# A looped ScalarE, lora_E on SyncE's queue, three idle matmuls and a moved pause in an AdaLoRA forward kernel

## The chip, the cores and the metric

The kernel runs on one core of a Trainium2 chip. Its time is the device time of one execution in microseconds (us): before the change the median of 3 runs is 161.67 us (161.62 to 162.06). A core has five engines that run by themselves and meet at semaphores: TensorE (PE in the profile, with its weight loads as PEld), VectorE (DVE), ScalarE (ACT), GpSimd (POOL) and SyncE (SP). SyncE and ScalarE issue transfers (DMAs) between the chip's main memory and the core's on-chip memory; 16 DMA engines carry them.

## The reference

```python
x_flat = x.reshape(-1, in_dim)          # x: 16 x 2048 x 256, f32
y = x_flat @ W                          # W: 256 x 256
lora_out = x_flat @ lora_A              # lora_A: 256 x 16
lora_out = lora_out * lora_E            # lora_E: 16
lora_out = lora_out @ lora_B            # lora_B: 16 x 256
y = y + scale * lora_out                # scale = 1.0
```

So 32768 rows of 256 numbers are read (33.5 MB), multiplied by a 256 x 256 matrix with a low-rank term added, and 33.5 MB are written.

## The kernel before, in words

The low-rank term is folded into the weights once: lora_A is transposed by TensorE (L171), scaled by lora_E on VectorE (L175), multiplied by lora_B (L180) and added to W, in bf16 (`weff`, L184). After that one multiplication by `weff` gives y.

The rows of x are cut into five blocks. A block of b rows a partition is a tile of 128 partitions x b x 256 in on-chip memory; `PLAN` gives b as 56, 56, 48, 48, 48. There is room for three blocks (three slots, of 56, 56 and 48 rows), and y is written over x in the same place, so blocks 3 and 4 can be loaded only after stores 0 and 1 have landed. A block is loaded in two or three pieces, each with its own semaphore, and stored by one transfer.

Work goes in 32 steps of 8 rows a partition (7 for each of the first two blocks, 6 for each of the rest). Step t is: VectorE rounds x to bf16 (`rounded`, L159); TensorE transposes it as 8 f32 blocks, two bf16 numbers in each f32 word (`transposed`, L198); VectorE copies the transposed block out of PSUM (`copied`, L163); TensorE multiplies it by `weff` in two halves of 8 matmuls (`multiplied`, L209); ScalarE copies each half out of PSUM over x (L232). TensorE runs its steps in a loop of 16 turns of two; ScalarE's 64 copies are written out one by one, each waiting for the count of finished halves in `s_m`.

All loads of x and all stores are issued by SyncE, in this order: W, load 0, load 1, load 2, store 0, store 1, load 3, load 4, store 2, store 3, store 4. Each store waits for ScalarE's copy of the block's last half (`s_y`); some issues wait for more: store 1 for 30 finished halves (`ISSUE_PRODUCTS`, L245), load 3 for store 0 and load 4 for store 1 to have landed, load 4 also for 20 transposed steps (`ISSUE_LOAD`, L250), store 3 for 29 (`ISSUE_STORE`, L243). ScalarE issues the three small loads of lora_A, lora_B and lora_E at the front.

VectorE holds the whole compute back once (`HOLD`, L151 to L158): ahead of step 16 it runs ten no-operations, waits until store 0 has landed, and then makes five copies into a spare tile, each waited for.

```python
HOLD = 16, 0, 5        # step, store that is waited for, spare copies
```

Of the kernel before, what the change touches and what calls it, by code (L numbers as in the profile page):

```python
# [4 lines left out]
PLAN = [56, 56, 48, 48, 48]  # L5

PIECES = {0: [16, 16, 24], 1: [16, 16, 24], 2: [24, 24], 3: [24, 24], 4: [24, 24]}

SLOTS = [56, 56, 48]
LEAD = 3  # L10
AFTER = {1: [3, 4]}

HOLD = 16, 0, 5


ISSUE_LOAD, ISSUE_STORE = {4: 20}, {3: 29}
ISSUE_PRODUCTS = {1: 30}

S, G = 8, 4
P = 128  # L20
FP32 = mybir.dt.float32
# [16 lines left out]
def kernel(tc, x, W, lora_A, lora_B, lora_E, scale, out):  # L38
    nc = tc.nc
    x_flat = x.flatten_outer_dims()  # L40
    out_flat = out.flatten_outer_dims()
    N, K = x_flat.shape
    M = out_flat.shape[1]
    R = lora_B.shape[0]
# [4 lines left out]
    steps = [(i, r) for i, b in enumerate(PLAN) for r in range(0, b, S)]  # L49
    NS = len(steps)  # L50
    assert NS % 2 == 0

    def rows_of(flat, i):
        b, r0 = PLAN[i], starts[i]
        return flat[r0:r0 + b * P, :].rearrange("(p b) k -> p b k", b=b)

    def sbuf(name, shape, dt):
        return nc.alloc_sbuf_tensor(name, shape, dt).ap()

    def psum(name, shape, dt):  # L60
        return nc.alloc_psum_tensor(name, shape, dt).ap()

    slots = [sbuf(f"xy{s}", [P, rows, K], FP32) for s, rows in enumerate(SLOTS)]
    a_sb = sbuf("a_sb", [P, KC, R], FP32)
    e_sb = sbuf("e_sb", [R, 1], FP32)
    w_sb = sbuf("w_sb", [P, KC, M], FP32)
    b_sb = sbuf("b_sb", [R, M], FP32)
    b_bf = sbuf("b_bf", [R, M], BF16)
# [3 lines left out]
    ident = sbuf("ident", [P, P], FP32)  # L72
# [7 lines left out]
    ps_y = [psum(f"psum_y{k}", [P, G, M], FP32) for k in range(2)]  # L80
# [4 lines left out]
    s_w, s_a, s_b, s_e = (Count(nc, f"s_{k}") for k in "wabe")  # L85

    pieces = {}
    for i, b in enumerate(PLAN):
# [1 line left out]
        pieces[i] = [(sum(parts[:j]), n) for j, n in enumerate(parts)]  # L90
    s_ld = {(i, r): Count(nc, f"s_ld{i}_{r}") for i in pieces for r, n in pieces[i]}
    s_st = [Count(nc, f"s_st{i}") for i in range(len(PLAN))]
    s_id, s_set, s_v, s_t, s_m, s_y = (
        Count(nc, k) for k in ("s_id", "s_set", "s_v", "s_t", "s_m", "s_y"))
    tick = nc.alloc_semaphore("tick")


# [2 lines left out]
    can_y = [[nc.alloc_semaphore(f"can_y{h}_{k}") for k in range(2)] for h in range(S // G)]  # L100

    def slot(i):
        return slots[i % LEAD][:, :PLAN[i], :]

    opening = []

    def transfer(queue, count, **aps):
        ins = queue.dma_start(**aps)
        for names in opening:
            names.add(ins.ins.name)  # L110
        count.by(ins, 16)

    def load(i):
        for r, n in pieces[i]:
            transfer(nc.sync, s_ld[i, r], out=slot(i)[:, r:r + n, :], in_=rows_of(x_flat, i)[:, r:r + n, :])

    def store(i):
        transfer(nc.sync, s_st[i], out=rows_of(out_flat, i), in_=slot(i))

    def spent(engine, count):  # L120
        engine.wait_ge(count.sem, count.total).then_inc(count.sem, -count.total)

    def take(sem):
        nc.tensor.wait_ge(sem, 1).then_inc(sem, -1)
# [4 lines left out]
    transfer(nc.sync, s_w, out=w_sb, in_=W.rearrange("(p c) m -> p c m", c=KC))  # L129
    transfer(nc.scalar, s_a, out=a_sb, in_=lora_A.rearrange("(p c) r -> p c r", c=KC))  # L130
    transfer(nc.scalar, s_b, out=b_sb, in_=lora_B)
    transfer(nc.scalar, s_e, out=e_sb, in_=lora_E[:, None])
    load(0)
    opening.clear()
    tc.close()
# [1 line left out]
    for i in range(1, LEAD):  # L137
# [5 lines left out]
        out=ident, in_=ident, compare_op=mybir.AluOpType.not_equal, fill=1.0, base=0,  # L143
# [3 lines left out]
    def rounded(t):  # L147
        i, r = steps[t]
        if (i, r) in s_ld:
            nc.vector.wait_ge(s_ld[i, r].sem, 16)  # L150
        if t == HOLD[0]:  # L151

            for _ in range(10):
                nc.vector.engine_nop()
            nc.vector.wait_ge(s_st[HOLD[1]].sem, 16)
            for _ in range(HOLD[2]):
                nc.vector.tensor_copy(out=spare, in_=slot(i)[:, r:r + 2 * S, :]).then_inc(tick, 1)  # L157
                nc.vector.wait_ge(tick, 1).then_inc(tick, -1)  # L158
        nc.vector.tensor_copy(out=xb[t % 2], in_=slot(i)[:, r:r + S, :]).then_inc(can_t[t % 2], 1)  # L159

    def copied(t):
        nc.vector.wait_ge(s_t.sem, t + 1)
        nc.vector.tensor_copy(out=xt[t % 2], in_=ps_xt[t % 2]).then_inc(can_m, 1)  # L163


    nc.vector.wait_ge(s_b.sem, 16)
    s_v.by(nc.vector.tensor_copy(out=b_bf, in_=b_sb))  # L167
    nc.tensor.wait_ge(s_a.sem, 16)
    nc.tensor.wait_ge(s_id.sem, 2)
    for c in range(KC):  # L170
# [4 lines left out]
    s_v.by(nc.vector.tensor_scalar(  # L175
        out=ate, in0=ps_at, scalar1=e_sb, scalar2=float(scale),
        op0=mybir.AluOpType.mult, op1=mybir.AluOpType.mult))
    nc.tensor.wait_ge(s_v.sem, 2)
    for c in range(KC):
        aeb_done = nc.tensor.matmul(ps_aeb[:, c, :], ate[:, c, :], b_bf, start=True, stop=True)  # L180
    s_set.by(aeb_done)
    nc.vector.wait_ge(s_w.sem, 16)
    nc.vector.wait_ge(s_set.sem, 2)
    s_v.by(nc.vector.tensor_add(out=weff, in0=w_sb, in1=ps_aeb))  # L184
    rounded(0)
    rounded(1)
    for t in range(NS):
        copied(t)
        if t + 2 < NS:
            rounded(t + 2)  # L190
# [12 lines left out]
    def multiplied(k):  # L203
        take(can_m)
        for h in range(S // G):
            nc.tensor.wait_ge(can_y[h][k], 1)
            for j in range(G):
                for c in range(KC):
                    done = nc.tensor.matmul(  # L209
                        ps_y[h][:, j, :], pairs[k][:, h * G + j, :, c], weff[:, c, :],  # L210
                        start=(c == 0), stop=(c == KC - 1))
                if j == 0:
                    done.then_inc(can_y[h][k], -1)
            done.then_inc(s_m.sem, 1)

    transposed(0)
    nc.tensor.wait_ge(s_v.sem, 3)
# [1 line left out]
    with nc.tensor.Fori(0, NS // 2):  # L219
        for k in range(2):  # L220
            transposed(1 - k)
            multiplied(k)
    s_t.total, s_m.total = NS + 1, NS * S // G

    for h in range(S // G):
        nc.scalar.sem_inc(can_y[h][0], 1)
    n = 0
    for i, r in [(i, r + g) for i, r in steps for g in range(0, S, G)]:
        n += 1
        nc.scalar.wait_ge(s_m.sem, n)  # L230
        t, h = divmod(n - 1, S // G)
        y = nc.scalar.copy(out=slot(i)[:, r:r + G, :], in_=ps_y[h])  # L232
        free = can_y[h][(t + 1) % 2]
        if r + G < PLAN[i]:
            y.then_inc(free, 1)
        else:
            done = s_y.by(y)
            if n < s_m.total:
                nc.scalar.wait_ge(s_y.sem, done)
                nc.scalar.sem_inc(free, 1)  # L240
            nc.sync.wait_ge(s_y.sem, done)
            if i in ISSUE_STORE:
                nc.sync.wait_ge(s_t.sem, ISSUE_STORE[i])  # L243
            if i in ISSUE_PRODUCTS:
                nc.sync.wait_ge(s_m.sem, ISSUE_PRODUCTS[i])  # L245
            store(i)
            for later in AFTER.get(i, []):
                nc.sync.wait_ge(s_st[later - LEAD].sem, 16)
                if later in ISSUE_LOAD:
                    nc.sync.wait_ge(s_t.sem, ISSUE_LOAD[later])  # L250
                load(later)


    for count in [s_a, s_id]:
# [1 line left out]
    spent(nc.tensor, s_v)  # L256
    for count in [s_b, s_e, s_w, s_set] + list(s_ld.values()):
        spent(nc.vector, count)
    spent(nc.scalar, s_m)
    nc.tensor.wait_ge(can_y[0][NS % 2], 1).then_inc(can_y[0][NS % 2], -1)  # L260
    for count in [s_y, s_t] + s_st:
        spent(nc.sync, count)

# [34 lines left out]
```

## Time and profile before

| what | value |
|---|---|
| median of 3 runs | 161.67 us |
| the profiled execution | 161.75 us |
| its span, first to last instruction | 160.4 us |
| moved | 67.42 MB, 420 GB/s over the span |
| busy: PE, DVE, ACT | 57%, 55%, 39% |
| VectorE waits for store 0 at the hold | 19.0 us, until 70.6 |
| first copy of ScalarE, last copy | from 16.4, from 131.1 us |

Times in the profile are counted from the start of the span. In the page's second part the span is cut into 40 slices of 4.0 us; a digit is the busy share of a slice in tenths, and GB/s is what the DMA engines moved. The third part has one row for each DMA queue: packets, megabytes, share of 16 engines' span; q1 is SyncE's queue, q10 is ScalarE's, q14 carries instructions. In a table by windows each row gives the stretch, its length, busy us and instructions (x) of PE, PEld, DVE, ACT and POOL, then the granted TensorE clock, the DMA share and GB/s. A row of waits reads: who waited, for whom, us in total, times, longest. A row of the timeline reads: start, us, engine, line, operation, how many.

### The profile page before, as it was taken

The numbers are of one execution on the slowest core, as the hardware profiler recorded it, in microseconds if no ns is written. First come the engines' busy times: TensorE is split into PE (matmuls) and PEld (weight loads), VectorE is DVE, ScalarE is ACT, GpSimd is POOL, SyncE is SP. The second block draws the span as 40 slices with busy tenths as digits, with TensorE's granted clock in tenths as the row PEclk, the third lists the DMA queues.
The fourth block names the chain that finished last, engine by engine and source line by source line (L and its number), as shares of the span: only waits on it lengthen the run. The fifth ranks groups of instructions, "written<-read, shape, count | busy, mean of one in ns | idle before, by whom it ended". The sixth has DMA issues, their size and how long they took to land. (4 is left out here: it accounts for less than half of the span.)

```text
span 160.4 us, 1883 instructions
## 1 busy us (share of the span) xinstructions
PE 91.8 (57%) x780; PEld 82.7 (52%) x780; DVE 87.9 (55%) x72; ACT 63.2 (39%) x65; POOL 0.7 (0%) x6
## 2 busy tenths in 40 slices
PE   0149999999999600000009999999999960000000
PEld 0028889999999500000008999999999950000000
DVE  0187769998988000039999669899898500000000
ACT  1100675868676700000001768686868670000000
POOL 1000000000000000000000000000000000000000
PEclk9999999999999975555555999999999999555555
DMA  5999999999999999999989999999999999999994
GB/s 179 409 433 447 429 415 433 449 435 411 466 404 392 458 457 457 457 443 457 415 386 382 423 404 460 411 455 423 496 404 404 466 453 429 404 417 490 429 429 196
DMA packets 2802, 67.42 MB, mean 420 GB/s; under 512 B 480, under 2 KB 496, under 8 KB 624
## 3 DMA queue, kind: packets, MB, share of 16 engines
q1 hardware_dynamic: 2592, 67.37, 98.0%
q10 hardware_dynamic: 208, 0.03, 0.2%
q14 instruction: 2, 0.02, 0.0%
HBM read 33.85 MB, written 33.55 MB: 420 GB/s over the span
## 5 line engine op out<-in xcount | busy, mean ns | idle before, releaser
L232 ACT COPY xy<-psum_y 128x1024 f32<-128x1024 f32 x64 | 61.9, 1017 | 65.5 <-PE psum_y L209 65.5
L209 PE MATMUL psum_y<-weff,xt 128*128 128x256 bf16 x512 | 63.7, 280 | 0.1
L209 PEld LDWEIGHTS psum_y<-weff,xt 128*128 128x128 bf16 x512 | 51.4, 101 | 7.1 <-issue 0.3
L198 PE MATMUL psum_xt<-ident,xb 128*128 128x128 f32 x264 | 36.8, 287 | 31.3 <-DVE xb L159 31.3
L198 PEld LDWEIGHTS psum_xt<-ident,xb 128*128 128x128 f32 x264 | 31.9, 148 | 32.7 <-DVE xb L159 32.3
L163 DVE COPY xt<-psum_xt 128x1024 f32<-128x1024 f32 x32 | 39.1, 1222 | 8.4 <-PE psum_xt L198 8.2
L159 DVE CAST xb<-xy 128x2048 bf16<-128x2048 f32 x32 | 38.9, 1220 | 3.7 <-DMA xy<-in_x_dram 3.4
L157 DVE CAST spare<-xy 128x4096 bf16<-128x4096 f32 x5 | 11.5, 2294 | 19.5 <-DMA out_dram<-xy 19.0
L167 DVE CAST b_bf<-b_sb 16x256 bf16<-16x256 f32 x1 | 0.3, 281 | 5.6 <-DMA b_sb<-in_lora_B_dram 5.6
L171 PE MATMUL psum_xt<-ident,a_sb 128*16 128x128 f32 x2 | 0.6, 396 | 4.2 <-POOL ident L142 4.2
L232 ACT ACT_TABLE_LOAD x1 | 1.3, 1283 | 3.5 <-PEq L136 3.5
L180 PE MATMUL psum_xt<-b_bf,ate 16*128 16x256 bf16 x2 | 0.6, 404 | 3.6 <-DVE ate L175 3.6
L171 PEld LDWEIGHTS psum_xt<-ident,a_sb 128*16 128x16 f32 x2 | 0.1, 90 | 4.2 <-DMA a_sb<-in_lora_A_dram 4.2
L180 PEld LDWEIGHTS psum_xt<-b_bf,ate 16*128 16x128 bf16 x2 | 0.1, 106 | 4.1 <-DVE ate L175 4.1
L175 DVE TENSOR_SCALAR ate<-psum_xt,e_sb 16x256 bf16<-16x256 f32 x1 | 0.5, 472 | 2.0 <-DMA e_sb<-in_lora_E_dram 2.0
L184 DVE TENSOR_TENSOR weff<-w_sb,psum_xt 128x512 bf16<-128x512 f32 x1 | 0.7, 689 | 0.8 <-PE psum_xt L180 0.8
L142 POOL TENSOR_SCALAR_AFFINE_SELECT ident<-ident 128x128 f32<-128x128 f32 x1 | 0.3, 294 | 0.2 <-POOL ident L140 0.2
L140 POOL MEMSET ident<- 128x128 f32 x1 | 0.2, 205 | 2.9 <-POOLq L136 2.9
L279 POOL MEMSET const-bfloat16-1.0<- 128x1 bf16 x1 | 0.1, 102 | 0.0
L279 POOL MEMSET const-uint8-127<- 128x1 uint8 x1 | 0.1, 102 | 0.0
L279 POOL MEMSET const-float32-0.0<- 128x1 f32 x1 | 0.1, 99 | 0.2 <-issue 0.2
L279 POOL MEMSET const-float32-1.0<- 128x1 f32 x1 | 0.1, 99 | 0.0
## 6 DMA issues: line engine op xcount, KB each, us to landing
xy<-in_x_dram SPq DMA_DIRECT2D x8, 3072.0 KB, 27.9
out_dram<-xy SPq DMA_DIRECT2D x3, 6144.0 KB, 28.2
out_dram<-xy SPq DMA_DIRECT2D x2, 7168.0 KB, 34.3
xy<-in_x_dram SPq DMA_DIRECT2D x4, 2048.0 KB, 17.8
w_sb<-in_W_dram SPq DMA_DIRECT2D x1, 256.0 KB, 3.0
a_sb<-in_lora_A_dram ACTq DMA_DIRECT2D x1, 16.0 KB, 3.1
b_sb<-in_lora_B_dram ACTq DMA_DIRECT2D x1, 16.0 KB, 4.4
e_sb<-in_lora_E_dram ACTq DMA_DIRECT2D x1, 0.1 KB, 6.2
```

The source lines that it names most:

```text
L142: s_id.by(nc.gpsimd.affine_select(out=ident, in_=ident, compare_op=mybir.AluOpType.not_equal, fill=1.0, base=0, pattern=[[-1, P]], channel ...
L157: nc.vector.tensor_copy(out=spare, in_=slot(i)[:, r:r + 2 * S, :]).then_inc(tick, 1)
L159: nc.vector.tensor_copy(out=xb[t % 2], in_=slot(i)[:, r:r + S, :]).then_inc(can_t[t % 2], 1)
L163: nc.vector.tensor_copy(out=xt[t % 2], in_=ps_xt[t % 2]).then_inc(can_m, 1)
L171: at_done = nc.tensor.transpose(ps_at[:, c, :], a_sb[:, c, :], ident)
L175: s_v.by(nc.vector.tensor_scalar(out=ate, in0=ps_at, scalar1=e_sb, scalar2=float(scale), op0=mybir.AluOpType.mult, op1=mybir.AluOpType.mult))
L180: aeb_done = nc.tensor.matmul(ps_aeb[:, c, :], ate[:, c, :], b_bf, start=True, stop=True)
L184: s_v.by(nc.vector.tensor_add(out=weff, in0=w_sb, in1=ps_aeb))
L198: done = nc.tensor.transpose(ps_xt[k][:, j, :], words[k][:, j, :], ident)
L209: done = nc.tensor.matmul(ps_y[h][:, j, :], pairs[k][:, h * G + j, :, c], weff[:, c, :], start=(c == 0), stop=(c == KC - 1))
L232: y = nc.scalar.copy(out=slot(i)[:, r:r + G, :], in_=ps_y[h])
L279: nc = _bacc.Bacc("TRN2", target_bir_lowering=False, num_devices=1)
```

## The change

- **ScalarE's copies loop over a ring.** The three slots become one tile of 160 rows (`RING`), in which block i starts at `AT[i]`: 0, 56, 112, 0, 48. ScalarE runs two loops, of 10 and 6 turns, each turn four copies (two steps), addressed by the turn's number. `s_m` is now taken down by one ahead of each copy by an instruction of its own. The last copy of a turn raises `last_y`, for which ScalarE waits; it then raises the semaphore that frees PSUM for TensorE and `s_y`, which now counts turns. SyncE's stores wait for the turn that holds the block's last row; block 0 ends in the middle of turn 4.
- **Store 1's extra wait** is no longer for 30 halves but for `s_hold`, which VectorE raises when it reaches the hold.
- **lora_E's load** is issued by SyncE, between W and load 0, no longer by ScalarE as its third. ScalarE copies lora_E to a tile that nothing reads (`e_copy`), ahead of its loops.
- **Three idle matmuls** of `ident` by W (128 x 128 by 128 x 512, f32) go to TensorE into a PSUM tile that is later overwritten: one ahead of the product for `weff`, two behind it.
- **The hold** stands ahead of step 17, which is the first of the second piece of block 2, with 24 no-operations and six spare copies.

```diff
-SLOTS = [56, 56, 48]
+RING, AT = 160, [0, 56, 112, 0, 48]
-HOLD = 16, 0, 5
+HOLD = 17, 0, 6
-ISSUE_PRODUCTS = {1: 30}
...
-    transfer(nc.scalar, s_e, out=e_sb, in_=lora_E[:, None])
+    transfer(nc.sync, s_e, out=e_sb, in_=lora_E[:, None])
     load(0)
...
         if t == HOLD[0]:
-            for _ in range(10):
+            nc.vector.sem_inc(s_hold, 1)
+            for _ in range(24):
                 nc.vector.engine_nop()
             nc.vector.wait_ge(s_st[HOLD[1]].sem, 16)
...
+    def idle(times):
+        for _ in range(times):
+            nc.tensor.matmul(ps_y[0][:, :2, :].rearrange("p g m -> p (g m)"), ident, w_sb[:, :, :].rearrange("p c m -> p (c m)"),
+                             start=True, stop=True)
...
+    nc.tensor.wait_ge(s_w.sem, 16)
+    idle(1)
     nc.tensor.wait_ge(s_v.sem, 2)
     for c in range(KC):
         aeb_done = nc.tensor.matmul(ps_aeb[:, c, :], ate[:, c, :], b_bf, start=True, stop=True)
     s_set.by(aeb_done)
+    idle(2)
...
+    nc.scalar.wait_ge(s_e.sem, 16)
+    nc.scalar.copy(out=e_copy, in_=e_sb)
...
-    for i, r in [(i, r + g) for i, r in steps for g in range(0, S, G)]:
-        n += 1
-        nc.scalar.wait_ge(s_m.sem, n)
-        t, h = divmod(n - 1, S // G)
-        y = nc.scalar.copy(out=slot(i)[:, r:r + G, :], in_=ps_y[h])
...
+    for turns in (RING // (2 * S), NS // 2 - RING // (2 * S)):
+        with nc.scalar.Fori(0, turns) as turn:
+            for k in range(2):
+                for h in range(S // G):
+                    nc.scalar.wait_ge(s_m, 1).then_inc(s_m, -1)
+                    first = turn * (2 * S) + (k * S + h * G)
+                    y = nc.scalar.copy(out=xy[:, bass.ds(first, G), :], in_=ps_y[h])
+                    y.then_inc(can_y[h][1] if k == 0 else can_y[0][0] if h == 0 else last_y, 1)
+            nc.scalar.wait_ge(last_y, 1).then_inc(last_y, -1)
+            nc.scalar.sem_inc(can_y[1][0], 1)
+            nc.scalar.sem_inc(s_y.sem, 1)
+    s_y.total = NS // 2
+    rows = 0
+    for i, b in enumerate(PLAN):
+        rows += b
+        nc.sync.wait_ge(s_y.sem, -(-rows // (2 * S)))
+        if i in ISSUE_STORE:
+            nc.sync.wait_ge(s_t.sem, ISSUE_STORE[i])
+        if i in AFTER:
+            nc.sync.wait_ge(s_hold, 1).then_inc(s_hold, -1)
+        store(i)
```

More of the change, by code (lines that the diff above doesn't have):

```diff
@@ L61, in psum @@
         return nc.alloc_psum_tensor(name, shape, dt).ap()
-    slots = [sbuf(f"xy{s}", [P, rows, K], FP32) for s, rows in enumerate(SLOTS)]
+    xy = sbuf("xy", [P, RING, K], FP32)
     a_sb = sbuf("a_sb", [P, KC, R], FP32)
     e_sb = sbuf("e_sb", [R, 1], FP32)
+    e_copy = sbuf("e_copy", [R, 1], FP32)
     w_sb = sbuf("w_sb", [P, KC, M], FP32)
@@ L92 @@
     s_st = [Count(nc, f"s_st{i}") for i in range(len(PLAN))]
-    s_id, s_set, s_v, s_t, s_m, s_y = (
-        Count(nc, k) for k in ("s_id", "s_set", "s_v", "s_t", "s_m", "s_y"))
+    s_id, s_set, s_v, s_t, s_y = (Count(nc, k) for k in ("s_id", "s_set", "s_v", "s_t", "s_y"))
+    s_m, last_y, s_hold = (nc.alloc_semaphore(k) for k in ("s_m", "last_y", "s_hold"))
     tick = nc.alloc_semaphore("tick")
@@ L102, in slot @@
     def slot(i):
-        return slots[i % LEAD][:, :PLAN[i], :]
+        return xy[:, AT[i]:AT[i] + PLAN[i], :]
     opening = []
@@ L213, in multiplied @@
                     done.then_inc(can_y[h][k], -1)
-            done.then_inc(s_m.sem, 1)
+            done.then_inc(s_m, 1)
     transposed(0)
@@ L222 @@
             multiplied(k)
-    s_t.total, s_m.total = NS + 1, NS * S // G
+    s_t.total = NS + 1
+    nc.scalar.wait_ge(s_e.sem, 16)
+    nc.scalar.copy(out=e_copy, in_=e_sb)
     for h in range(S // G):
         nc.scalar.sem_inc(can_y[h][0], 1)
-    n = 0
-    for i, r in [(i, r + g) for i, r in steps for g in range(0, S, G)]:
-        n += 1
-        nc.scalar.wait_ge(s_m.sem, n)
-        t, h = divmod(n - 1, S // G)
[L232 to L251, printed above, removed]
@@ new lines @@
+    s_y.total = NS // 2
[8 more added lines that the diff above has]
+        store(i)
+        for later in AFTER.get(i, []):
+            nc.sync.wait_ge(s_st[later - LEAD].sem, 16)
+            if later in ISSUE_LOAD:
+                nc.sync.wait_ge(s_t.sem, ISSUE_LOAD[later])
+            load(later)
@@ L258 @@
         spent(nc.vector, count)
-    spent(nc.scalar, s_m)
-    nc.tensor.wait_ge(can_y[0][NS % 2], 1).then_inc(can_y[0][NS % 2], -1)
+    for h in range(S // G):
+        nc.tensor.wait_ge(can_y[h][NS % 2], 1).then_inc(can_y[h][NS % 2], -1)
     for count in [s_y, s_t] + s_st:
```

## The prediction

> **What bounds the kernel now.** I read the page's slices and queue rows first, because a kernel that moves 67 MB may be bound by its transfers alone.
>
> ```profile
> DMA  5999999999999999999989999999999999999994
> GB/s 179 409 433 447 429 415 433 449 435 411 466 404 392 458 457 457 457 443 457 415 386 382 423 404 460 411 455 423 496 404 404 466 453 429 404 417 490 429 429 196
> q1 hardware_dynamic: 2592, 67.37, 98.0%
> q14 instruction: 2, 0.02, 0.0%
> ```
>
> The reader is to see that the DMA engines are at 9 tenths or more in 37 of 40 slices, the other three being the first, the last and one 8, and that queue q1 (all that SyncE issues) fills 98% of 16 engines' span. No compute engine passes 57%. The page's chain of waits ends at 132 us with ScalarE's last copy, 28 us before the end: it follows compute, and compute is not what ends last. Next, the windows by stage, to ask whether compute slows the transfers:
>
> ```profile
> 34.00:54.00 20.00, 20.00 (x186) 18.61 (x184) 15.90 (x14) 14.46 (x16) 0.00 (x0) 1.00 1.01 424
> 54.00:70.60 16.60, 0.75 (x7) 0.42 (x5) 0.00 (x0) 1.84 (x2) 0.00 (x0) 0.62 1.02 442
> 84.00:101.00 17.00, 16.91 (x135) 15.22 (x136) 14.07 (x14) 9.74 (x10) 0.00 (x0) 0.86 1.01 433
> 101.00:117.00 16.00, 16.00 (x149) 14.89 (x147) 14.67 (x13) 11.58 (x12) 0.00 (x0) 1.00 1.01 434
> ```
>
> The last columns are granted clock, DMA share and GB/s. With compute at full pace (84 to 117 us) the queue moves 433 to 434 GB/s, without it (54 to 70.6) 442; packets are counted whole where they start, so a few per cent between windows mean little. The landings are sharper. Issue plus time to landing gives: first piece of load 0 at 9.3 us, store 0 at 70.6, store 1 at 87.8, load 3 at 95.0 and 102.4, load 4 at 109.7 and 117.0, store 2 at 131.5, store 3 at 146.0, store 4 at 160.4. A 3 MB piece of loads 3 and 4 takes 7.3 us, each of the last three stores 14.4 to 14.5: 431 to 436 GB/s, compute or not. So the end is set by when the first byte moves, by the bytes, and by whether the queue ever runs dry. Third, what SyncE waits for:
>
> ```profile
> SPq L108 <- ACT xy L232: 46.6, 3, 29.1
> SPq L250 <- PE psum_xt L198: 23.3, 1, 23.3
> SPq L245 <- PE psum_y L209: 19.5, 1, 19.5
> SPq L243 <- PE psum_xt L198: 17.8, 1, 17.8
> SPq L108 <- DMA out_dram<-xy: 15.4, 1, 15.4
> ```
>
> These waits look large, but each ends before the queue is empty. The transfer ahead of each issue, from the landings above, gives the **slack**: store 0 issued at 34.9, load 2 landing at 53.6 (18.7 us); store 1 at 54.8 against 70.6 (15.8); load 4 at 95.3 against 102.4 (7.1); store 2 at 100.7 against 117.0 (16.3); store 3 at 118.9 against 131.5 (12.6); store 4 at 132.2 against 146.0 (13.8). Anything done to compute must cost over 7 us to be seen.
>
> **The change, part by part.**
>
> *The hold.* VectorE's pause moves from ahead of step 16 to ahead of step 17, and its spare copies go from five to six.
>
> ```profile
> 70.61 12.05 DVE L157 CAST spare<-xy 128x4096 bf16<-128x4096 f32 x5 [18.97 <-DMA out_dram<-xy]
> ```
>
> One copy with the wait on its own completion is 12.05 / 5 = 2.41 us, so the hold ends at 70.6 + 6 x 2.41 = 85.1 instead of 82.7, 2.4 later. One step fewer remains after it. A step on TensorE in the chain is 0.87 + 1.75 = 2.62 us. Net 2.4 - 2.6 = -0.2 us: load 4's gate (20 transposed steps) and the later stores' gates stay where they are, within 1 us, against slacks of 7.1 and more. Price 0. The copies read memory beside stores, but store 1 took 17.2 us for 7.34 MB (427 GB/s) against 17.0 for store 0, so one copy more costs at most (17.2 - 17.0) / 5 = 0.04 us. The 14 more no-operations run at VectorE while it waits 19.0 us for store 0; ten of them took under 0.2 us. Price 0.
>
> *Store 1's gate.* It waited for 30 half-step products; now for seven turns of ScalarE and for VectorE's signal at the hold, which stands behind the landing of load 2 (53.6) and the copy of step 15 (about 54.3). So about 54.5 instead of 54.8; behind it in SyncE's order wait loads 3 and 4, which need store 0 at 70.6 anyway. Price 0; without cover it would cost one us per us past 70.6.
>
> *Store 0's gate.* Progress is now counted by two steps, so store 0 waits for eight steps, not seven: 34.9 + 2.6 = 37.5, slack 16. The other blocks end on whole turns. Price 0.
>
> *ScalarE's loop.* Each half-step gets a semaphore instruction of its own, and each turn of four copies waits for its last copy, signals twice and branches back.
>
> ```profile
> L232 ACT COPY xy<-psum_y 128x1024 f32<-128x1024 f32 x64 | 61.9, 1017 | 65.5 <-PE psum_y L209 65.5
> ```
>
> Four copies are 4 x 1.02 = 4.07 us in a turn that TensorE gives 2 x 2.62 = 5.24: 1.17 us are free. The nearest row for a wait on one's own completion is VectorE's, 2.41 - 2.29 = 0.12 us; TensorE's own loop shows no gap between steps in the chain. I take 0.5 us a turn, from 0 to 1.2; hidden by TensorE, and beyond that by the slack of 13.8. The unrolled copies go away, and with them perhaps one of the two 8 KB instruction packets in the span (309 ns each, on one DMA engine of 16). Were that engine the last, this would gain 0.3; it is one of 16, so 0, with ends -0.3 and 0.
>
> *Idle matmuls.* No row shows an f32 matmul of 512 columns. [...] VectorE next waits for the third piece of load 0 until 21.5, and store 0 has 16 us of slack. Price 0.
>
> *lora_E.* Its issue (0.44 us on ScalarE's queue) goes to SyncE, between W and the first piece of x: x is issued at 1.61 instead of 1.17, and everything behind it in that queue too. This is the only edit that touches the path. The first microseconds in slices of 0.1 us:
>
> ```profile
> DMA  0093953179999998040069993499993379999093
> GB/s 0 0 102 41 164 102 127 61 259 388 328 392 394 635 1876 351 22 166 0 0 184 553 338 707 164 174 338 655 492 819 164 164 328 655 492 492 492 0 492 164
> DMA packets 384, 1.33 MB, mean 332 GB/s; under 512 B 177, under 2 KB 193, under 8 KB 321
> ```
>
> W was issued at 0.74 and moves from 1.8, so 1.07 us from issue to first packet. The spike at 3.0 us is x's first 16 KB packet on most engines; until then they carry W and lora_A. At the lag of W, x issued at 1.61 is ready at 2.7, before the engines are free: delay 0, plus some 0.05 for lora_E's 16 tiny packets in line. The upper end is the whole issue, 0.44. The lower end: the window moves 332 GB/s instead of 436, but 0.2 us of it precede any packet; in the 2 us from 3.6 small packets of lora_B and lora_E stand among x's, and I put what could be won there at 0.4. I take +0.05, by W's row, the nearest, on the same queue. [...]
>
> *Switch from load to store.* The last piece of load 2 took 53.6 - 45.9 = 7.7 us where the others take 7.3; no row says why. The changed kernel has the same transfers in the same order there: 0, with ends -0.4 and +0.4.
>
> **Sum.** The profiled execution took 161.75 us: 160.4 of span, 1.35 around it, 0.08 above the median. 161.75 + 0.05 = 161.80, or 161.7 on the median of 161.67.
>
> **Rivals.** *Slower by the front (C).* x is late by lora_E's issue and its packets: 0.44 + 0.1 to 0.2, so 162.3. For it: x's first packet is only 0.2 to 0.3 us behind the estimate of its being ready. Against: W's lag. A delay begins once x's lag from issue exceeds W's 1.07 by 0.3 and is whole at 0.75; it decides only if it is whole and the packets cost 0.05 beside it.
>
> *Slower by ScalarE's loop (B).* A turn would have to cost so much that the last store comes late: from about 88 us eight turns remain, and store 4 must be issued by about 145, so the turn must pass 57 / 8 = 7.1 us, 3 above its four copies. At 8 us the last issue is at 152, 7 us late: 168. Against it: TensorE's loop turns without a gap and the instruction queue carries two packets in all. [...]
>
> *Faster (A).* The small packets leave x's way at the front (-0.4), or the switch loss of 0.4 goes, with an instruction packet fewer (up to -0.3): 161.1. For it: the 332 GB/s at the front. Against: lora_B's packets stay, and the switch is not edited.
>
> **How the numbers follow.** A measurement of this kernel tells a change from none at about 0.3%, 0.49 us. Forecast (all hidden, 161.7): 0.50, its own range 161.3 to 162.1. A: 0.23. C, or a second switch loss of 0.4 with part of C: 0.23. B: 0.04. So faster 0.23, same 0.50, slower 0.27. The range leaves out B and the outer parts of A and C: from 161.67 - 0.7 = 161.0 (the front's gain with an instruction packet) to 161.67 + 0.6 + 0.1 = 162.4.
>
> **What the profile of the changed kernel would show.** The spike of x's first packets at 3.0 us if lora_E is free, at 3.3 to 3.5 if C holds, and the first piece landing at 9.3 or 9.7. The first spare copy at 70.6, the hold's end at 85. ScalarE's copies 5.2 us a turn, and its last near 132; past 145 would be B. Stores landing 14.4 to 14.5 us apart at the end. The forecast is wrong if any two of the last five landings stand further apart, or if the first piece lands over 0.5 us from 9.3.

## The result, and the profile after

The changed kernel is slower: 163.94 us median (163.89 to 164.11) against 161.69, a ratio of 1.0134 with a 95% interval from 1.0119 to 1.015. The forecast was 161.7. The profiled execution took 164.11 us with a span of 162.8.

The page of the changed kernel, its slices and queue rows:

```profile
DMA  4999999999999899999998999999998999999991
GB/s 149 350 431 433 459 397 447 453 417 441 423 429 483 380 409 425 451 451 437 451 451 366 417 453 417 441 429 441 489 423 387 459 459 423 399 435 483 423 399 60
q1 hardware_dynamic: 2624, 67.37, 96.9%
q14 instruction: 1, 0.01, 0.0%
```

The transfers still bound the kernel: q1 fills 96.9% of a span that is 2.4 us longer. Two slices stand out. The second (4 to 8 us) moves 350 GB/s where it moved 409, and the last moves 60: by the trace's arrivals 11 of the 16 engines are done by 160.2 us, five still work. One of the two instruction packets is gone; the page does not say which engine's.

The first microseconds, from 1.6 to 5.6 in slices of 0.1, of the changed kernel (a packet counts whole in the slice in which it starts, so a 0 does not mean that the engines stood still):

```profile
DMA  0900025599899999195070579090679939879739
GB/s 0 61 0 0 0 102 207 188 384 305 323 372 383 612 816 428 46 363 164 0 164 0 164 328 819 0 655 0 164 328 492 492 164 655 164 328 655 328 164 655
DMA packets 404, 1.15 MB, mean 287 GB/s; under 512 B 208, under 2 KB 224, under 8 KB 352
```

Before, the spike of x's first packets at 3.0 us read 635, 1876, 351. It is still at 3.0, so x is not late as a whole. But it reads 612, 816, 428: not all engines start together. From 3.4 to 5.4 us 13.3 of the 16 engines had a packet under way on average, against 14.8 before, and of the first 128 packets of 16 KB 29 took over 0.8 us, against 3. Before, 15 of the first 16 of them start between 2.93 and 3.12 us; in the changed kernel the 16 starts run from 2.98 to 4.00.

SyncE's first issues, from the timelines, with start and length in us; first the kernel before, then the changed one:

```profile
0.74 0.38 SPq L108 DMA_DIRECT2D w_sb<-in_W_dram  x1
1.17 4.61 SPq L108 DMA_DIRECT2D xy<-in_x_dram  x8
```

```profile
0.74 0.38 SPq L107 DMA_DIRECT2D w_sb<-in_W_dram  x1
1.18 0.42 SPq L107 DMA_DIRECT2D e_sb<-in_lora_E_dram  x1
1.65 5.33 SPq L107 DMA_DIRECT2D xy<-in_x_dram  x8
```

The rows of x's first piece among the issues, issued at 1.17 us before and at 1.65 us in the changed kernel, each with its time to landing, in the same order:

```profile
xy<-in_x_dram SPq DMA_DIRECT2D x1, 2048.0 KB, 8.1
```

```profile
xy<-in_x_dram SPq DMA_DIRECT2D x1, 2048.0 KB, 9.3
```

It landed at 10.95 instead of 9.3. The trace records 16 arrivals for each transfer, one for each of the 16 DMA engines as I read them, and the landing is the last of them: for this piece of the changed kernel they run from 8.96 to 10.95. I call the time from the first of them to the last the *spread*:

| landing, us: first / middle / last engine | before | changed |
|---|---|---|
| first piece of load 0 | 8.47 / 8.65 / 9.26, spread 0.8 | 8.96 / 9.19 / 10.95, spread 2.0 |
| third piece of load 0 | 20.66 / 20.91 / 21.49, spread 0.8 | 21.18 / 21.44 / 23.15, spread 2.0 |
| last piece of load 4 | 115.71 / 116.07 / 116.95, spread 1.25 | 116.06 / 116.33 / 118.57, spread 2.5 |
| store 4, the end | 159.12 / 159.60 / 160.41, spread 1.3 | 159.47 / 159.78 / 162.74, spread 3.3 |

The middle engine is 0.2 to 0.5 us later than before, all through. The last one is 1.7 us later after the first piece, 1.6 after load 4 and 2.3 at the end: what was lost by 11 us the last engine never made up, and the rest came after load 4. The lag was taken along: the spread is 1.99 us after the first piece, 1.97 after the third and 1.99 after the last of load 1 (45.55 to 47.54).

The rest of the chain of events is as forecast. The hold and ScalarE's copies in the changed kernel, from its timeline and its groups:

```profile
72.53 14.49 DVE L157 CAST spare<-xy 128x4096 bf16<-128x4096 f32 x6 [16.61 <-DMA out_dram<-xy]
L246 ACT COPY xy<-psum_y 128x1024 f32 x64 | 61.7, 1017 | 66.8 <-ACTq L244 66.8
```

Six spare copies take 14.49 us (2.41 each), and start at 72.5 because store 0 lands 1.9 us late. SyncE's waits in the changed kernel:

```profile
SPq L107 <- ACTq L250: 51.2, 3, 32.5
SPq L264 <- PE psum_xt L207: 22.4, 1, 22.4
SPq L257 <- PE psum_xt L207: 17.4, 1, 17.4
SPq L107 <- DMA out_dram<-xy: 16.5, 1, 16.5
SPq L259 <- SPq L259: 15.8, 1, 15.8
```

Four of them are within 5 us of their length before (store 1's new wait, L259, takes 15.8 where the old one took 19.5), and they are as harmless: store 1 is issued at 55.7, load 4 at 96.4, store 4 at 134.0, all with the transfer ahead of them still under way (store 0 to 72.5, load 3 to 104, store 3 to 148.2).

### The profile page after: what moved, and what is told of

Read it like the earlier page. It is cut to its first block, busy times and chain, and to the rows that moved or that the text cites. A ratio compares the mean times of both kernels' runs of the same rounds, so it can differ in the third digit from the quotient of the medians.

```text
span 162.8 us, 2135 instructions
## 1 busy us (share of the span) xinstructions
PE 93.9 (58%) x786; PEld 81.6 (50%) x786; DVE 90.2 (55%) x73; ACT 63.2 (39%) x66; POOL 0.8 (1%) x6
## 3 DMA queue, kind: packets, MB, share of 16 engines
q1 hardware_dynamic: 2624, 67.37, 96.9%
## 5 line engine op out<-in xcount | busy, mean ns | idle before, releaser
L246 ACT COPY xy<-psum_y 128x1024 f32 x64 | 61.7, 1017 | 66.8 <-ACTq L244 66.8
L218 PE MATMUL psum_y<-weff,xt 128*128 128x256 bf16 x512 | 61.8, 274 | 0.7 <-PEq L123 0.3
L207 PE MATMUL psum_xt<-ident,xb 128*128 128x128 f32 x264 | 35.4, 278 | 33.2 <-DVE xb L159 33.2
L218 PEld LDWEIGHTS psum_y<-weff,xt 128*128 128x128 bf16 x512 | 50.2, 99 | 7.2 <-issue 1.5
L207 PEld LDWEIGHTS psum_xt<-ident,xb 128*128 128x128 f32 x264 | 30.3, 143 | 35.6 <-DVE xb L159 35.3
L157 DVE CAST spare<-xy 128x4096 bf16<-128x4096 f32 x6 | 13.8, 2294 | 17.3 <-DMA out_dram<-xy 16.6
L167 PE MATMUL psum_y<-w_sb,ident 128*128 128x512 f32 x6 | 4.9, 950 | 0.0
L167 PEld LDWEIGHTS psum_y<-w_sb,ident 128*128 128x128 f32 x6 | 1.7, 321 | 1.5 <-issue 1.4
```

Source lines behind the costliest of these rows:

```text
L167: nc.tensor.matmul(ps_y[0][:, :2, :].rearrange("p g m -> p (g m)"), ident, w_sb[:, :, :].rearrange("p c m -> p (c m)"), start=True, stop=True)
L207: done = nc.tensor.transpose(ps_xt[k][:, j, :], words[k][:, j, :], ident)
L218: done = nc.tensor.matmul(ps_y[h][:, j, :], pairs[k][:, h * G + j, :, c], weff[:, c, :], start=(c == 0), stop=(c == KC - 1))
L246: y = nc.scalar.copy(out=xy[:, bass.ds(first, G), :], in_=ps_y[h])
```

## The experiments

Times are medians; ratios are to the kernel before, measured on the same chip, with 95% intervals. "Lag" is the time from W's issue to the issue of x's first piece on SyncE. Theories: **F**, the front, lora_E's new place; **R**, the rest of the change; within F, **G** (x issued late lets engines run empty) against **P** (tiny packets) and **N** (any small transfer there).

**Only lora_E taken back** (changed kernel).

```diff
-    transfer(nc.sync, s_e, out=e_sb, in_=lora_E[:, None])
+    transfer(nc.scalar, s_e, out=e_sb, in_=lora_E[:, None])
```

> The changed kernel with one part undone: lora_E is again ScalarE's third load; loop, ring, hold, idle matmuls stay. Theory F (the whole loss of 2.2 us is lora_E standing ahead of x in SyncE's queue): 161.7, first piece of x landing at 9.3 us, the spread of the 16 landings 0.8 us. Theory R (the loss is the rest of the change, the idle matmuls reading W beside the landing x, or the loop): 163.5 to 164, and the spread stays at 2.0 us.

162.24 us, ratio 1.0025 (1.0003 to 1.0047). The first piece lands at 9.1 us, with a spread of 0.57. Nearly all of the loss is gone: this is for F, and R falls as the main cause. Some 0.2% is left; two of the ten runs stand out, at 162.94 and 163.38.

**Only lora_E moved** (kernel before, the same line the other way).

> The kernel before with lora_E's load issued by SyncE between W and x, nothing else. Theory F: 163.9, first piece landing at 10.9, spread 2.0. Theory R: 161.7 to 162.1, the first piece at 9.3 to 9.7.

163.85 us, 1.0113 (1.0073 to 1.0153); the first piece lands at 10.75 us, with a spread of 2.09. This one line gives the loss by itself. From 3.2 to 7.2 us this kernel moves

```profile
DMA packets 77, 1.26 MB, mean 315 GB/s; under 512 B 0, under 2 KB 0, under 8 KB 0
```

where the kernel before moves, in the same window,

```profile
DMA packets 159, 1.49 MB, mean 373 GB/s; under 512 B 52, under 2 KB 68, under 8 KB 69
```

There are no small packets at all in the slower window: they are done before it begins.

**W in two halves** (kernel before).

```diff
-    transfer(nc.sync, s_w, out=w_sb, in_=W.rearrange("(p c) m -> p c m", c=KC))
+    for p in (0, P // 2):
+        transfer(nc.sync, s_w, out=w_sb[p:p + P // 2], in_=w_rows[p:p + P // 2])
```

> The kernel before with W loaded in two halves of 64 partitions, two issues on SyncE; lora_E stays on ScalarE. x is issued 0.44 us later, as in the changed kernel, but no tiny packets stand ahead of it. Within theory F this parts F1 (x's late issue does it: 163.9, spread 2.0) from F2 (the tiny packets of lora_E in x's queue do it: 161.7 to 162.1, spread 0.8 to 1.0).

162.68 us, 1.0042 (1.0025 to 1.0059), in ten runs from 162.3 to 164.33. x is issued at 1.96, later than in the changed kernel, and yet nine runs lose only 0.4 to 0.9 us. The tenth, which was the profiled one, has a spread of 2.7 and 164.33 us: the stall can come without lora_E in the queue. It is not free of tiny packets, because each transfer on this queue ends in 16 packets of 4 bytes (288 for its 18 transfers in the kernel before), and W in two halves brings 16 more. I had expected a clean answer and this was none; in hindsight W itself was later here, its second half issued at 1.34.

**No idle matmuls** (changed kernel, the two calls of `idle` taken out).

> The changed kernel without its three idle matmuls; lora_E stays on SyncE. Theory F: 163.9 as with them, spread 2.0. Theory R in the form that the idle matmuls' reads of W hold up the landing x: 161.7 to 162.5, spread near 0.8.

163.57 us, 1.012 (1.0079 to 1.0161), spread 2.2. The idle matmuls are not the cause.

**lora_E ahead of W** (kernel before; lora_E, W, x on SyncE).

```diff
+    transfer(nc.sync, s_e, out=e_sb, in_=lora_E[:, None])
     transfer(nc.sync, s_w, out=w_sb, in_=W.rearrange("(p c) m -> p c m", c=KC))
```

> The kernel before with lora_E issued by SyncE ahead of W: lora_E, W, x. x is issued 0.44 us late as in the changed kernel, but W is late too, so x still follows W in the engines without a gap. Theory G (the DMA engines stall where they run empty ahead of x): 162.1, the 0.44 alone, spread of the first piece's landings 0.8. Theory P (lora_E's tiny packets in the queue ahead of x): about 163.9, spread 2.0.

162.38 us, 1.0031 (1.0018 to 1.0043), spread 0.53. x is issued at 1.646, exactly as late as in the slow version; the stall is gone and the issue's 0.45 us is about what is left. That is for G and against P; N, which was not yet named, says the same.

**lora_E behind x's first piece** (kernel before).

```diff
         for r, n in pieces[i]:
             transfer(nc.sync, s_ld[i, r], out=slot(i)[:, r:r + n, :], in_=rows_of(x_flat, i)[:, r:r + n, :])
+            if (i, r) == (0, 0):
+                transfer(nc.sync, s_e, out=e_sb, in_=lora_E[:, None])
```

> The kernel before with lora_E issued by SyncE behind the first piece of x: W, x, lora_E, x. The first piece is issued when it was. Theories G and P both: first piece at 9.3 with a spread of 0.8; P in its wider form (tiny packets ahead of any piece) a loss of 1.5 us or more at the second piece; G: 161.5 to 161.8. The setup ends about 11 us instead of 9.8, which the slack of 16 us covers.

161.80 us, 0.9998 (0.9986 to 1.0009); the first piece lands at 8.6 us, with a spread of 0.23. Tiny packets inside x's queue cost nothing, so P in its wider form falls. There is no gain either, though the first piece lands 0.65 us earlier than in the kernel before and the front is more even than in any other version: at the end the spread is 1.4 us, against 1.3.

**One tiny descriptor** (kernel before, with an added 64-byte load between W and x).

```diff
+    transfer(nc.sync, s_one, out=one_sb, in_=lora_E[None, :])
```

> The kernel before with an added load of lora_E as one row of 64 bytes, one descriptor, on SyncE between W and x; nothing reads it, lora_E's own load stays on ScalarE. x is 0.44 us late; only one engine gets a tiny packet. Theory G: 163.9, spread 2.0, as the changed kernel. Theory P: 162.1, spread 0.8 to 1.0.

162.49 us, 1.0053 (1.0026 to 1.008), and two kinds of runs: eight of ten from 161.83 to 162.93, two at 163.75 and 163.84. The issue is shorter here (0.32 us), x goes out at 1.553: neither theory's figure, but a first hint of an edge. The profiled run is one of the eight.

**A short pause** (kernel before, six increments of an unused semaphore on SyncE between W and x).

```diff
+    for _ in range(6):
+        nc.sync.sem_inc(s_idle, 1)
```

> The kernel before with six semaphore increments on SyncE between W and x, which nothing waits for: x is issued about 0.45 us late and no transfer is added. Theory G: 163.9, spread 2.0. Theory P: 162.1, spread 0.8 to 1.0.

161.94 us, 1.0012 (0.9998 to 1.0026), spread 0.45. x is issued 0.36 us late, at 1.529, and its first packet starts at 2.96: this lateness is free, as the forecast had it. By itself this spoke against G.

**A long pause** (the same, 14 increments).

> The kernel before with 14 semaphore increments on SyncE between W and x instead of six: x is issued about 0.85 us late, later than lora_E makes it (0.47), and no transfer is added. If lateness past 0.4 us brings the stall (G'): 163.5 to 164, spread 2.0. If not (P, N): 162.1 to 162.4, the part of the lateness that W no longer covers, spread under 1.0.

163.73 us, 1.0123 (1.0079 to 1.0168), from 162.78 to 164.49; in the profiled run a spread of 1.3 at the first piece and 2.1 at the end. No transfer was added, so lateness alone can bring a loss of this size; neither P nor N is needed for it. In this kernel, from 3.2 to 7.2 us:

```profile
DMA  9968699000000999330979090979395399373099
DMA packets 112, 1.43 MB, mean 357 GB/s; under 512 B 24, under 2 KB 25, under 8 KB 25
```

The loss is made up differently, though. At the first piece the middle engine lands 0.7 us later than in the kernel before, and one engine is over 0.75 us behind it; with lora_E between W and x the middle one is 0.4 us later and five are 1.2 to 1.7 behind it. Of the 112 packets behind x's first 16, 3 took over 0.8 us here, 11 with lora_E there. A pause of lora_E's own length, to a lag of 0.91, was not run. So it is not shown how much of lora_E's loss is the lag alone and how much needs a small transfer in that place (N).

**lora_E, then a pause** (kernel before, lora_E between W and x, eight increments behind it).

> The kernel before with lora_E on SyncE between W and x and eight semaphore increments between lora_E and x: the tiny packets are done before x's first are ready. P and N in the form that the small packets must stand directly ahead of x: 162.3 to 162.6, spread under 1.0. In the form that they upset the queue as such, or under G': 163.9 or more, spread 2.0.

163.72 us, 1.0088 (1.0059 to 1.0118), in five runs of two kinds: three from 163.72 to 164.37, two at 162.63 and 162.77. Parting the tiny packets from x does not take the loss away, but with the longest lag of all it is not in full in every run.

**lora_B in lora_E's place** (kernel before; W, lora_B, x on SyncE, lora_E as ScalarE's second).

> The kernel before with lora_B (16 rows of 1 KB) issued by SyncE between W and x, lora_E in lora_B's place on ScalarE: as many packets ahead of x as lora_E brings, but 1 KB each. P (the 4-byte size): 162.0 to 162.3, spread under 1.0. N (any 16-row transfer there): 163.9, spread 2.0.

163.78 us, 1.0118 (1.01 to 1.0135), spread 1.89. Sixteen packets of 1 KB do what sixteen of 4 bytes do, so P falls: it is not the 4 bytes. From 3.2 to 7.2 us:

```profile
DMA packets 106, 1.22 MB, mean 305 GB/s; under 512 B 28, under 2 KB 31, under 8 KB 32
```

**lora_E ahead of W in the changed kernel** (the cure tried where the loss was; **Q** is G put sharply, that x's queue must not run empty behind W, **L** that x must go out by about 1.6 whatever stands ahead).

> The changed kernel with lora_E still on SyncE's queue but ahead of W: lora_E, W, x. x is issued exactly as late as in the changed kernel, but only 0.46 us behind W instead of 0.91. Theory Q (the loss comes where x's queue has run empty between W and x; lateness as such costs only itself): 162.4 to 162.7, spread of the first piece's landings under 1.0. Theory L (x must be issued by about 1.6, whatever is ahead of it): 163.9, spread 2.0.

162.59 us, 1.0042 (1.0027 to 1.0057), spread 0.76. x is issued at 1.644 in it and at 1.650 in the changed kernel; the lag differs, 0.46 against 0.91, and nothing stands between W and x. L falls. From 3.2 to 7.2 us it moves, against 322 GB/s in the changed kernel,

```profile
DMA packets 143, 1.62 MB, mean 404 GB/s; under 512 B 18, under 2 KB 18, under 8 KB 48
```

**x ahead of W** (kernel before; first piece of x, then W, on SyncE).

> The kernel before with the first piece of x issued ahead of W on SyncE. Theory Q: nothing stands ahead of x that it could be late behind, so no spread (under 0.9), and x's packets start at 1.8 instead of 3.0 while W's 0.7 us of transfer moves behind the first piece: 161.2 to 161.6, faster than both. Theory L: the same. If the front's length doesn't reach the end: 161.8.

161.73 us, 0.9997 (0.9988 to 1.0006). The first piece landed at 8.1 instead of 9.3, W at 8.9. There is no stall, but no gain: by the third piece the middle engine lands at 20.85 us, against 20.91 in the kernel before, as if W's transfer were only moved behind the first piece. Nothing stood ahead of this x in its queue, and its first 16 packets took 0.7 to 1.4 us each, yet the spread is 0.5: an empty queue by itself does not bring the stall. My 161.2 to 161.6 was wrong, and nothing I tried beats the kernel before.

**What is left of the change without the stall.** Three versions of the changed kernel, all with lora_E behind x's first piece.

> The changed kernel with lora_E still on SyncE's queue, but behind the first piece of x. If the place ahead of x is all that loses: 161.7 to 162.0, the first piece at 9.3 at the latest, spread under 0.9. If the rest of the change costs 0.3% of its own, as the run with lora_E back on ScalarE hinted (162.24 against 161.93): 162.2.

162.18 us, 1.0021 (1.001 to 1.0031), spread 0.40.

> The changed kernel with lora_E behind the first piece of x, and without the idle matmuls. The version with them took 162.18, 0.2% over before. If the idle matmuls are that 0.2%: 161.8. If not: 162.2.

162.13 us, 1.0018 (1.0009 to 1.0027).

> The changed kernel with lora_E behind the first piece of x, and the hold as before: ahead of step 16, ten no-operations, five spare copies. If the moved hold is the 0.2% that is left: 161.8. If the loop on ScalarE or the idle matmuls are: 162.2.

162.03 us, 1.0013 (1.0004 to 1.0022). Between 0.1 and 0.2% stays in each, so the idle matmuls are not it; the moved hold may be part, but the intervals overlap, and ScalarE's loop and the ring were never taken back alone. It stays open. In the three profiled runs load 4 lands at 116.6 to 117.0 us, against 116.95 in the kernel before, and store 2 lands 15.17, 15.03 and 14.62 us behind it, against 14.54. The kernel before with lora_E between W and x has 15.37 there, so this does not belong to the rest of the change alone. Together lora_E's 1.0113 and 1.0021 give the 1.0134 of the whole change.

Ordered by lag, the versions fall apart into two groups. "Begun" is how many of x's 16 KB packets had started when W's last packet ended; it and the spread are of the profiled run.

| version | lag, us | x issued | begun | spread | median |
|---|---|---|---|---|---|
| before | 0.43 | 1.17 | 15 | 0.8 | 161.7 to 161.9 |
| lora_E taken back in the changed kernel | 0.43 | 1.17 | 14 | 0.6 | 162.24 |
| lora_E behind x's first piece | 0.44 | 1.17 | 13 | 0.2 | 161.80 |
| lora_E ahead of W | 0.46 | 1.65 | 16 | 0.5 | 162.38 |
| the same in the changed kernel | 0.46 | 1.64 | 14 | 0.8 | 162.59 |
| W in two halves, from the second | 0.63 | 1.96 | 13 | 2.7 | 162.68, this run 164.33 |
| short pause | 0.79 | 1.53 | 15 | 0.45 | 161.94 |
| one tiny descriptor | 0.81 | 1.55 | 12 | 0.6 | 162.49, two of ten near 163.8 |
| lora_E between W and x | 0.91 | 1.65 | 7 | 2.1 | 163.85 |
| changed kernel | 0.91 | 1.65 | 8 | 2.0 | 163.94 |
| changed kernel, no idle matmuls | 0.91 | 1.65 | 7 | 2.2 | 163.57 |
| lora_B between | 0.91 | 1.65 | 7 | 1.9 | 163.78 |
| long pause | 1.26 | 2.00 | 0 | 1.3 | 163.73 |
| lora_E, then pause | 1.39 | 2.12 | 0 | 1.35 | 163.72, two of five near 162.7 |

Up to a lag of 0.81 us 12 to 16 of x's packets have started when W's last one ends; at 0.91 it is 7 or 8, and after the longer pauses none. W in two halves does not fit: its profiled run has the stall with 13 begun. The packet records do not name their engine, so that the slow engines are those that had run empty is not shown. Why some engines stay slow for some 4 us, and why it is five of 16 in the changed kernel and not all, no run here shows.

## Why the prediction was wrong, point by point

- **What bounds the kernel**: right. The transfers set the end, and none of SyncE's waits let the queue run dry later on. What I read past is that "the queue" is 16 engines, whose arrivals the trace records one by one; the span of 162.8 us ended with the slowest one's, at 162.74. The 0.8 us of spread in the kernel before was already in the trace and I summed as if they moved as one. Both signs that I had named came: the first piece landed 1.7 us from 9.3, and store 2 landed 15.1 us behind load 4, not 14.4 to 14.5.
- **The hold, store 0's and store 1's gates, ScalarE's loop**: hidden, as forecast, to within 0.2%. Store 0 was issued at 39.5 us, not 37.5, and load 2 covered it until 55.5. The hold took 14.49 us for six copies, as forecast; ScalarE idles 0.7 us between its pairs of copies, as before, so its loop hides behind TensorE, and rival B did not come (its 168 should be 168.7 by its own terms, 161.7 and 7 us; nothing hung on it). Where 0.1 to 0.2% of 162 us remains I had 0.
- **Idle matmuls**: 4.9 us for the three, which no row of the kernel before gave, and hidden all the same: taking them out changed nothing measurable, with the stall (ratio 1.012, whose interval holds the changed kernel's 1.0134) or without (162.13 against 162.18).
- **lora_E**: this is the step that failed. Its term was +0.05, between -0.4 and +0.44; alone it measured 1.0113, about +1.8 us. Half of the reasoning held: in the versions with the stall x's first packet started 1.1 to 1.3 us after the issue, near W's 1.07, and a short pause of 0.36 us was free. lora_E brought 32 packets of 4 bytes to the queue (320 in the changed kernel, 288 before), 9 ns each, so 0.02 us an engine on average, less than the 0.05 put down for them. But W's 1.07 is the time to the first packet of the first engine, and I took it for all 16. Where no packet of W was left ahead of x, its first 16 packets started 1.0 to 1.7 us after the issue (x ahead of W) or 1.2 to 1.9 (long pause). By these two rows an x issued at 1.65 reaches the last engine at 3.4 to 3.5, an estimate, while W's last packet ended at 3.33 in the changed kernel. The margin that I called 0.2 to 0.3 us held for the first engine only: the pause used 0.36 and cost nothing, lora_E used 0.47 and went over the edge. And the upper end was set at the issue's own length, on the thought that a late transfer can lose no more than its lateness: five engines fell 0.8 to 1.8 us behind the middle one on top of it. Why they did stays open.
- **The issue's own length**, the upper end of that term (0.44 on the median of 161.67), would have made 162.1. The order lora_E, W, x shows that figure nearly (162.38); the order W, lora_E, x does not (163.85). The measurement decides: where in the queue the issue is put counts for more than its length.
- **Rival C** named the right place and the right direction with 0.44 + 0.1 to 0.2; its 0.6 us was a third of the 1.8 that lora_E alone cost.

## What to carry to other kernels

In a kernel that its transfers bound, read landings engine by engine: here the span of 162.8 us ended with the slowest engine's last arrival, at 162.74, the middle one's was at 159.78. The 1.7 us that the last engine lost at the front were still missing at the end, while 0.65 us won there (lora_E behind x's first piece) did not reach it. When a queue starts with a short load (here W) and a long one (x), time a further small load ahead of both and behind the first piece of the long one before you put it between them. Here the same load of 16 rows cost 1.8 us between them, 0.5 ahead of both and 0 behind the first piece. When a step leaves a margin of a few tenths of a microsecond, bound what happens beyond the margin by an experiment and not by the step's own length.

## What the runs showed of the hardware that I had not expected

- The cost of issuing x late behind W rises steeply between lags of 0.79 and 0.91 us: 0.1% on one side, 0.9 to 1.2% on the other, and both kinds of runs at 0.81. It is no rule for every run: beyond 0.91 three of nine runs lost only 0.8 to 1.0 us, and W in two halves had the stall once in ten at 0.63. At 0.91 a small transfer stood between W and x each time.
- In the changed kernel most of x's first packets of 16 KB take about 0.61 us as before, but 29 of the first 128 took 0.8 to 1.3 us, the last of these from 6.8 us, against 3 before.
- Increments of a semaphore on SyncE cost about 0.06 us each (0.36 for six, 0.83 for 14), and a transfer of one 64-byte packet took 0.32 us to issue where 16 rows took 0.42.
- The first 16 packets of x did not start at once: with nothing ahead of x in its queue its first 16 packets started over a stretch of 0.7 us (1.75 to 2.47, x ahead of W).
